# Both context units at the head of a bidirectional DeltaNet scan, and the context projection between its passes, on one Trainium2 core

## The chip, the core and the metric

The kernel runs on one core of a Trainium2 chip. The core has five engines with a queue of instructions each: TensorE (PE, matrix products; its weight loads are listed apart as PEld), VectorE (DVE), ScalarE (ACT), GpSimd (POOL) and SyncE (SP). Each engine takes its own queue in order and waits on semaphores for the others. All loads and stores between memory and the core's SBUF are issued on SP's queue, one behind the other. The metric is the device time of one execution in microseconds (us).

## The reference

One layer of a hybrid backbone over two sequences: 128 context tokens and 2048 latent tokens, width 1024, 4 heads of 128. Cut to what matters (the function names are those of the reference):

```python
def gated_delta_chunked(q, k, v, g, beta, s0):          # per head, chunks of 64 tokens
    ...
    sol = lax.linalg.triangular_solve(a_mat + jnp.eye(DN_CHUNK, dtype=f32), rhs, ...)
    ...
    def step(S, xs):
        qd, kd, u_c, w_c, qk_c, gl = xs
        v_new = u_c - jnp.einsum('bhck,bhkv->bhcv', w_c, S)
        o = jnp.einsum('bhck,bhkv->bhcv', qd, S) + jnp.einsum('bhcs,bhsv->bhcv', qk_c, v_new)
        S = S * jnp.exp(gl)[..., None, None] + jnp.einsum('bhck,bhcv->bhkv', kd, v_new)
        return S, o
def mixer(h, s0, ...):
    ...
    o_a, s_new = delta_bidir(q, k, v, g2, beta2, s0)     # o_forward + flip(o_backward)
    o_a = rmsnorm(o_a, o_norm_l) * jax.nn.silu(gate.reshape(B, T, H_A, DV))
    u = jax.nn.gelu(u)
    vg = layernorm_noaffine(jax.nn.gelu(vg).reshape(B, n_chunks, CHUNK_MLP, G_B, C_B))
    mixed = jnp.einsum('gts,bnsgc->bntgc', ws_l, vg) + bs_l.T[None, None, :, :, None]
    o_b = u * mixed.reshape(B, T, D_B).astype(u.dtype)
    out = jnp.concatenate([o_a.reshape(B, T, D_A).astype(h.dtype), o_b.astype(h.dtype)], axis=-1)
    return out @ w_out_l, s_new
def block(x, s0, mod, n_chunks, ...):
    h = rmsnorm(x, norm_mix_l) * (1.0 + sc1) + sh1
    o, s_new = mixer(h, s0, n_chunks, ...)
    x = x + ga1 * o
    h = rmsnorm(x, norm_ffn_l) * (1.0 + sc2) + sh2
    x = x + ga2 * (jnp.square(jax.nn.relu(h @ w_ff1_l)) @ w_ff2_l)
    return x, s_new
```

The context starts both directions from a zero state and its two final states are an output. The latents start each direction from a given state (`state_delta`), so the context's scan and the latents' scan do not depend on each other. The context's layer output is an output too.

## The kernel before

The 2176 tokens are 17 tiles of 128 (`NT`): tile 0 is the context, tiles 1 to 16 are the latents. Products that need full precision are made of three matrix products (`mm3`, lines 217 to 219): a factor is split into a high half H, cast on ACT, and a low half L, the difference, taken on DVE; the three are H x H, H x L and L x H. For weights the cast is line 191 and the difference line 192; line 190 scales the raw weight where it has a scale.

The kernel has three phases.

The first, to about 455 us, makes the modulation, the normed input, the projections to q, k and v, the convolution, and writes q, k, v, the products of k with k and q with k, the gates' exponents and the two halves of the input to memory.

The second, the scan, from about 455 to about 1294 us, is where the change is. It works on 34 units, each one tile in one direction. Before the change their order is: tiles 0 to 16 forward (units 0 to 16), tile 0 backward (unit 17), tiles 16 down to 1 backward (units 18 to 33). A unit has

- loads: `prep_loads` (gb, the row of exponents, by line 935; KK and QK), issued about three units ahead, and `scan_loads` (kT, qT, kt, vt, eg);
- a preparation (`prep`), which needs nothing of other units: the decay masks E and Es (ACT lines 977 and 978, two selects on POOL), KK (DVE line 990, POOL line 992), its half-precision copy AH (ACT line 995), X (DVE lines 996, 997), Y, the transpose of X (PE line 1003, copied by ACT on line 1005), and then five rounds of doubling the inverse, each of which is PE line 1025 (from Y), P on DVE (line 1029), PE lines 1038 and 1040 (from P), and copies of Y and X on ACT (1041, 1042). P has its fixed part written from `identq` (line 1028) in the units of tile 0 only, since later units of the same direction overwrite the same half;
- a chain step (`scan`) that hangs on the state S of the unit before: kt scaled (ACT 1093), vt, vn, the new state (`quad` on line 952, then line 1119 on DVE), and the output o (lines 1129 to 1136). A forward unit stores o to memory, a backward unit adds the stored forward part.

Both of the context's units and the first latent unit of each direction begin anew: behind units 0 and 17, `after` stores the context's final state and loads `state_delta` into a buffer of S, of which there are two.

Between the matrix products of units stand fillers. In the forward pass they are the rest of the mixer for each tile (`f2_steps`): the gate projection "g", and the gMLP's "v" and "u" (8 weight blocks of three products each, 24 products for a tile and part, tile "pm"/"pj"), their activation functions (from line 1159; the gate is computed on ACT and DVE and stored), the statistics, and the spatial product (line 1213 and its neighbours). The gates of the first four tiles (`HT`) are made before the scan. Weights of v and u are loaded and split about then too. In the backward pass the fillers are the output projection of the tile just finished (`o_steps`: norm, lines 1265 to 1273; transposes, 1286; the halves oH and oL; 48 products with the weights `w_out`, in tile "pj"; the residual, 1309 and 1310) and, for tiles above 8, the normed input of the MLP. `w_out` is loaded, scaled and split in 16 pieces near the end of the forward pass, in times 17.58 to 18.3.

The order is written down as events with a time, in units: `at(time, step)` sets one, `spread` spaces several evenly, and unit i's steps lie around time i. The events are sorted by time and emitted. A filler's first product is held behind the latest chain or preparation product. A planner then sets each engine's order with its own costs, so that the written times and the order on an engine agree only roughly. `NF` is the number of filler steps that are put ahead of the scan instead of being spread, at times -12 and -8; before the change it is 46. The fillers' sequence is: gates of tiles 0 to 3; v and u of tiles 0 to 3; g, v and u of tiles 4 to 14; then the last two tiles. Each step's inputs hH and hL are loaded one visit ahead. Staging tiles for weights come from a pool of four ("raw", `NS`); `part` is a temporary of the MLP's input, five buffers.

The third phase, from about 1294 us, is the MLP with weights combined on the fly and streamed (lines 1431 and 1437). The change does not touch it.

## Time and profile before

| | us |
|---|---|
| median of 3 runs | 2711.76 |
| fastest, slowest run | 2704.84, 2714.13 |
| profiled execution: device time | 2707.53 |
| profiled execution: span of the trace | 2705.8 |
| PE busy in the span | 2632.3 (97%) |
| DVE busy | 1868.0 (69%) |
| ACT busy | 1246.1 (46%) |

PE's busy time by stage, from windows of the trace:

| stage | length, us | PE busy, us | DVE busy, us | granted PE clock |
|---|---|---|---|---|
| first phase, 0 to 455 | 455 | 445.78 | 297.37 | 1.00 |
| forward pass, 455 to 914 | 459 | 439.12 | 347.81 | 0.98 |
| around the turn, 914 to 959 | 45 | 41.22 | 39.00 | 0.89 |
| backward pass, 959 to 1294 | 335 | 318.89 | 268.51 | 0.99 |
| MLP, 1294 to 2705 | 1411 | 1387.31 | 915.27 | 0.99 |

How to read a profile line: "L1025" is line 1025 of the kernel, followed by the engine, the operation, the tile written <- the tiles read, and the shape. A line of waits reads "engine, tile, line <- what it waited for: idle us in all, how often, longest". In a line of time order the first number is the start in us, the second the duration, and in square brackets stands the idle time ahead with what ended it. The granted clock is the share of full speed that PE was given: at 0.5 the same product takes twice as long. Busy time of PE at a low clock is therefore time lost as well.

### The profile page before, as it was taken

What the parts mean: (1) busy time and instruction counts of PE and PEld (TensorE: products, weight loads), DVE (VectorE), ACT (ScalarE), POOL (GpSimd) and SP (SyncE); (2) the same over time, 40 slices, a digit from 0 to 9 for tenths busy, and PEclk for the clock granted to TensorE, in tenths of its full rate; (3) what the DMA queues carried; (4) which work ended last, traced back from release to release, by engine and by line L of the source; (5) the groups of instructions that cost most, each with busy time, mean ns of one, the idle gap of its engine ahead of it and who ended that gap; (6) DMA issues with size and microseconds to landing.
All of it is one profiled execution on the core that took longest, in us unless ns stands there. A gap on an engine that the chain in (4) does not pass through costs nothing.

```text
span 2705.8 us, 45189 instructions
## 1 busy us (share of the span) xinstructions
PE 2632.3 (97%) x15698; PEld 2196.5 (81%) x15698; DVE 1868.0 (69%) x3909; ACT 1246.1 (46%) x3092; POOL 228.2 (8%) x448
## 2 busy tenths in 40 slices
PE   8999998999999999999999999999999999999998
PEld 5999997788887787778888778888888787788887
DVE  5867656877777978985677857565565556775874
ACT  4655555555555667763355533332342432232441
POOL 3111213111111111110000000000000000000000
PEclk9999999999999999999999999999999999999999
DMA  8867539555555657875887786433459979776772
GB/s 296 279 199 223 185 115 294 179 159 155 163 162 172 212 180 245 268 263 175 286 234 232 213 299 206 123 102 109 117 174 371 326 262 308 267 239 216 233 258 91
DMA packets 569387, 580.91 MB, mean 215 GB/s; under 512 B 35692, under 2 KB 401692, under 8 KB 565574
## 3 DMA queue, kind: packets, MB, share of 16 engines
q1 hardware_dynamic: 569158, 578.03, 66.5%
q8 instruction: 123, 2.02, 0.3%
q14 instruction: 106, 0.87, 0.1%
HBM read 398.14 MB, written 179.74 MB: 214 GB/s over the span
## 4 chain that ended last, share of the span: by engine, by line
PE 82%; DMA 7%; DVE 6%; issue 2%; ACT 2%; SPq 1%; POOL 0%; DVEq 0%; POOLq 0%; ACTq 0%
PE f L219 16%; PE f L217 16%; PE f L218 16%; PE pj L217 6%; PE pj L219 6%; PE pj L218 6%; PE pd L952 3%; PE pm L217 1%; DMA qT<-qT_d 1%; PE pm L218 1%; PE pm L219 1%; PE pt L568 1%; PE pd L1129 1%; PE pd L1130 1%; PE pt L528 1%
## 5 line engine op out<-in xcount | busy, mean ns | idle before, releaser
L219 PE MATMUL f<-hop,zL 128*128 128x512 f32 x960 | 377.9, 394 | 1.7 <-DVE zL L1431 1.7
L217 PE MATMUL f<-hop,zH 128*128 128x512 f32 x960 | 377.6, 394 | 1.2 <-ACT zH L1437 1.2
L218 PE MATMUL f<-hop,zH 128*128 128x512 f32 x960 | 378.0, 394 | 0.0
L217 PE MATMUL f<-hop,wH 128*128 128x512 f32 x896 | 356.2, 398 | 5.8 <-ACT wH L1437 5.8
L219 PE MATMUL f<-hop,wL 128*128 128x512 f32 x896 | 352.2, 393 | 0.0
L218 PE MATMUL f<-hop,wH 128*128 128x512 f32 x896 | 352.0, 393 | 0.0
L1437 ACT CAST zH<-zraw 128x512 fp32r<-128x512 f32 x240 | 147.1, 620 | 299.2 <-DVE zraw L1431 91.9
L219 PEld LDWEIGHTS f<-hop,zL 128*128 128x128 f32 x960 | 180.9, 188 | 45.0 <-DVE zL L1431 3.5
L217 PEld LDWEIGHTS f<-hop,zH 128*128 128x128 f32 x960 | 180.7, 188 | 44.7 <-ACT zH L1437 2.9
L218 PEld LDWEIGHTS f<-hop,zH 128*128 128x128 f32 x960 | 180.6, 188 | 40.9
L1431 DVE TENSOR_TENSOR zL<-zraw,zH 128x512 fp32r<-128x512 f32 x240 | 162.6, 687 | 68.2 <-ACT zH L1437 50.8
L217 PEld LDWEIGHTS f<-hop,wH 128*128 128x128 f32 x896 | 169.4, 189 | 40.9 <-ACT wH L1437 6.2
L219 PEld LDWEIGHTS f<-hop,wL 128*128 128x128 f32 x896 | 169.0, 189 | 38.0 <-DVE wL L1431 0.3
L218 PEld LDWEIGHTS f<-hop,wH 128*128 128x128 f32 x896 | 169.4, 189 | 35.2
L217 PE MATMUL pj<-kH,wH 128*128 128x386 f32 (+2 forms) x568 | 191.0, 339 | 0.3 <-DVE kH L466 0.3
L219 PE MATMUL pj<-kH,wL 128*128 128x386 f32 (+2 forms) x568 | 190.6, 336 | 0.0
L218 PE MATMUL pj<-kL,wH 128*128 128x386 f32 (+2 forms) x568 | 189.8, 334 | 0.0
L176 POOL TENSOR_TENSOR r<-rsq,nhalf 128x1 f32<-128x1 f32 (+1 forms) x38 | 23.6, 621 | 1516.4 <-DVE rsq L175 1516.4
L1431 DVE TENSOR_TENSOR wL<-raw,wH 128x512 fp32r<-128x512 f32 x112 | 76.1, 687 | 76.0 <-ACT wH L1437 75.0
L516 DVE SCALAR_TENSOR_TENSOR cv<-pj,vec,cv 128x384 f32<-128x384 f32 (+2 forms) x164 | 87.1, 539 | 59.9 <-ACT cv L513 58.5
L217 PEld LDWEIGHTS pj<-kH,wH 128*128 128x128 f32 x568 | 107.5, 190 | 4.8 <-issue 4.2
L217 PE MATMUL pj<-wH,hH 128*128 128x512 f32 x248 | 110.1, 444 | 0.0
(398 smaller groups left out, 6090.2 us busy)
## 6 DMA issues: line engine op xcount, KB each, us to landing
zraw<-z_d SPq DMA_DIRECT2D x212, 256.0 KB
raw<-in_w_ff_dram SPq DMA_DIRECT2D x128, 256.0 KB
hop<-hop_d SPq DMA_DIRECT2D x28, 1024.0 KB
z_d<-c SPq DMA_DIRECT2D x96, 256.0 KB
zraw<-s_d SPq DMA_DIRECT2D x96, 256.0 KB
raw<-in_w_mod_dram SPq DMA_DIRECT2D x80, 256.0 KB
r<-in_w_ff_dram SPq DMA_DIRECT2D x80, 256.0 KB
s_d<-s SPq DMA_DIRECT2D x64, 256.0 KB
```

What stands on the lines that cost most here:

```text
L176: G.tensor_tensor(out=out, in0=t[:np_, :n], in1=nhalf[:np_, :n], op=ALU.pow)
L217: T.matmul(ps, lh, rh, start=first and i == 0, stop=False, skip_group_check=more)
L218: T.matmul(ps, lh, rl, start=False, stop=False, skip_group_check=more)
L219: T.matmul(ps, ll, rh, start=False, stop=last and i == n - 1, skip_group_check=more)
L516: V.scalar_tensor_tensor(out=cv[:, o : o + m], in0=ps[:, s + sh : s + sh + m], scalar=convw[:, w, j : j + 1], in1=cv[:, o : o + m], op0=AL ...
L528: T.transpose(pq[:, i * P : (i + 1) * P], u["x2"][:, i * P : (i + 1) * P], ident)
L568: T.matmul(ps[:, i * P : (i + 1) * P], kTt[:, i * P : (i + 1) * P], rhs[:, i * P : (i + 1) * P], start=True, stop=True)
L952: T.matmul(p[:, h, :], lhs[:, h, :], rhs[:, h, :], start=True, stop=True)
L1129: T.matmul(p[:, h, :], u["qT"][:, h, :], s[:, h, :], start=True, stop=False)
L1130: T.matmul(p[:, h, :], u["QK"][:, h, :], u["vn"][:, h, :], start=s is None, stop=True)
L1431: V.tensor_tensor(out=out, in0=a, in1=b, op=op)
L1437: A.copy(h, src)
```

## The change

- The order of units becomes: tile 0 forward, tile 0 backward, tiles 1 to 16 forward, tiles 16 to 1 backward. `unit` gets two flags: `fresh` (units 0, 1, 2 and 18) writes the fixed part of P anew, because the direction turns there; `last` (tile 16 forward, tile 1 backward) leaves out the state update, whose result nobody reads.
- Tile 0's forward output stays in SBUF; its backward unit adds it and stores the sum, which the output projection loads again.
- `after` only stores the two context states; `first_state` loads `state_delta` for units 2 and 18. S has three buffers instead of two, `part` four instead of five.
- The context's output projection (`o_loads`, `o_steps` of unit 1) is written at 17.3 to 18.8, between the passes; it was at 17 to 19.66, as that of unit 17.
- The fillers' sequence becomes: gates of tiles 0 to 3; gates, then v, then u of tiles 4 and 5; g, v and u of tiles 6 to 14; v and u of tiles 0 to 3; the last two tiles as before. `NF` becomes 62. The loads of tile 4's and 5's input are at -11.5 and -9.5, the loads of unit 0 at -12.5 instead of -10.

```diff
-NF = 46
+NF = 62
...
-        def unit(t, d):
+        def unit(t, d, fresh=False, last=False):
...
-                    if t == 0:
+                    if fresh:
                         V.tensor_copy(pms[s], identq)
...
                 s = u["s"]
+                if last:
+                    return
                 p = pd()
                 quad(p, u["kt"], u["vn"])
-                sn = q32("S", 2)
+                sn = q32("S", 3)
...
-                o = q32("o", 2)
-                if d == 0:
+                u["o"] = o = q32("o", 2)
+                if t == 0 and d:
+                    V.tensor_tensor(out=o, in0=p, in1=units[0]["o"], op=ALU.add)
+                    store(out=of_d[0:P, :].rearrange("p (h d) -> p h d", h=H), in_=o)
+                elif d == 0:
                     A.copy(o, p)
+                    if t == 0:
+                        return
...
-        units = [unit(t, 0) for t in range(NT)] + [unit(t, 1) for t in [0] + list(range(NT - 1, 0, -1))]
+        units = [unit(0, 0, True), unit(0, 1, True)] + [unit(t, 0, t == 1, t == NT - 1) for t in range(1, NT)]
+        units += [unit(t, 1, t == NT - 1, t == 1) for t in range(NT - 1, 0, -1)]
...
-            return fp.tile([P, 512], F32, tag="part", name=name, bufs=5)
+            return fp.tile([P, 512], F32, tag="part", name=name, bufs=4)
...
+            if t == 0:
+                u["o"] = u["of"].rearrange("p (h d) -> p h d", h=H)
...
         def after(i):
 
-            d = 0 if i == 0 else 1
-            store(out=new_state[0, 0, d].rearrange("h k v -> k h v"), in_=units[i]["sn"])
-            s0 = q32("S", 2)
+            store(out=new_state[0, 0, i].rearrange("h k v -> k h v"), in_=units[i]["sn"])
+
+        def first_state(i, d):
+            units[i]["s0"] = s0 = q32("S", 3)
             load(out=s0, in_=state_delta[0, 0, d].rearrange("h k v -> k h v"))
-            units[i + 1]["s0"] = s0
...
-            at(i - 3 if i > PL else -10, u["prep_loads"])
+            at(i - 3 if i > PL else -12.5, u["prep_loads"])
...
-            if i >= NT:
+            if i > NT:
                 at(i, lambda u=u: o_loads(u))
...
-        for n, (t, gi) in enumerate([(t, "g") for t in range(HT)] + [(t, gi) for t in range(HT) for gi in "vu"]
-                                    + [(t, gi) for t in range(HT, NT - 2) for gi in "gvu"]
+        visits = [4, 5] + list(range(6, NT - 2)) + list(range(HT)) + [NT - 2, NT - 1]
+        after_visit = dict(zip(visits, visits[1:]))
+        for n, (t, gi) in enumerate([(t, "g") for t in range(HT)] + [(t, gi) for gi in "gvu" for t in (4, 5)]
+                                    + [(t, gi) for t in range(6, NT - 2) for gi in "gvu"]
+                                    + [(t, gi) for t in range(HT) for gi in "vu"]
                                     + [(NT - 2, "g"), (NT - 1, "g")]
                                     + [(t, gi) for t in (NT - 2, NT - 1) for gi in "vu"]):
...
-        at(-9, f2[0][0])
+        at(-11.5, f2[4][0])
+        at(-9.5, f2[5][0])
...
+        at(1, lambda: first_state(2, 0))
+        at(NT + 0.5, lambda: first_state(NT + 1, 1))
+        at(NT + 0.3, lambda: o_loads(units[1]))
+        first, second = o_steps(units[1])
+        spread(NT + 0.8, NT + 1.1, first, "fill")
+        spread(NT + 1.1, NT + 1.8, second, "fill")
```

More of the change, by code (lines that the diff above doesn't have):

```diff
@@ L1136, in _ @@
                     V.tensor_tensor(out=o, in0=p, in1=u["of"].rearrange("p (h d) -> p h d", h=H), op=ALU.add)
-                    u["o"] = o
             u["t"], u["d"] = t, d
@@ L1336, in g @@
                 if "s" not in u:
-                    u["s"] = None if i in (0, NT) else units[i - 1]["sn"] if i not in (1, NT + 1) else u["s0"]
+                    u["s"] = None if i < 2 else units[i - 1]["sn"] if i not in (2, NT + 1) else u["s0"]
                 f()
@@ L1357, in hybrid_step @@
             spread(i + w[2], i + w[3], [scan_step(i, f) for f in u["scan"]], "chain")
-            if i in (0, NT):
+            if i < 2:
                 at(i + w[2] + (w[3] - w[2]) * 0.7, lambda i=i: after(i))
-            if i >= NT:
+            if i > NT:
                 at(i, lambda u=u: o_loads(u))
@@ L1375, in hybrid_step @@
             main, later = f2[t][1][gi]
-            if gi == "v" and t + 1 < NT - 1 or gi == "g" and t == NT - 2:
-                flat.append((KT * n - 0.5, f2[t + 1][0]))
+            if gi == "v" and t not in (4, 5, NT - 2, NT - 1) or (t, gi) in ((5, "u"), (NT - 2, "g")):
+                flat.append((KT * n - 0.5, f2[after_visit[t]][0]))
             flat += [(KT * n + j, st) for j, st in enumerate(main)]
```

## The prediction

> **What bounds the kernel now.** I read the page first, then the stage windows, the waits of PE, and the orders in time of PE, ACT, DVE, POOL and SP around the two places that the windows single out.
>
> ```profile
> span 2705.8 us, 45189 instructions
> PE 2632.3 (97%) x15698; PEld 2196.5 (81%) x15698; DVE 1868.0 (69%) x3909; ACT 1246.1 (46%) x3092; POOL 228.2 (8%) x448
> 500.00:850.00 350.00, 344.62 (x2948) 285.26 (x2947) 258.53 (x745) 190.09 (x508) 44.61 (x58) 1.00 0.52 161
> 461.00:464.50 3.50, 1.16 (x7) 0.56 (x6) 3.16 (x6) 3.50 (x9) 1.66 (x2) 1.00 1.07 374
> 464.50:482.30 17.80, 10.50 (x56) 6.71 (x56) 15.20 (x40) 11.51 (x31) 7.47 (x6) 0.52 0.85 288
> 914.30:933.50 19.20, 16.54 (x147) 14.54 (x145) 18.84 (x59) 13.23 (x41) 3.90 (x5) 0.73 0.54 173
> 919.75:922.50 2.75, 1.08 (x21) 0.80 (x21) 2.75 (x8) 2.75 (x13) 0.51 (x1) 1.00 1.04 335
> 922.50:933.00 10.50, 9.50 (x77) 8.72 (x77) 10.14 (x40) 4.79 (x16) 3.39 (x5) 0.51 0.40 125
> 933.00:940.00 7.00, 6.14 (x71) 5.59 (x69) 6.94 (x21) 5.69 (x20) 0.00 (x0) 1.00 0.56 169
> ```
>
> PE is busy 97% of the span, so only its idle time, its slow time and removed work can be won. The windows list busy time of PE, weight loads, DVE, ACT, POOL, then the granted PE clock and the DMA share. The long forward stretch loses 350 - 344.6 = 5.4 us in 350. Two places lose far more. At the **start of the scan** (461 to 482.3) PE idles 2.34 + 7.30 us, and its 10.50 busy us run at clock 0.52, so 10.50 x 0.48 = 5.0 us are lost on speed: 14.7 us. At the **turn between the passes** (919.75 to 940) idle is 1.67 + 1.00 + 0.86 and the slow clock costs 9.50 x 0.49 = 4.7: 8.2 us. The change touches both.
>
> ```profile
> PE pd L1025 <- ACT Y L1005: 2.8, 1, 2.8
> PE pd L1038 <- DVE P L1029: 2.3, 3, 1.2
> PE pd L1025 <- ACT Y L1041: 1.0, 1, 1.0
> PE pm L218 <- DVE wL L192: 1.9, 2, 1.6
> PE pm L217 <- ACT wH L191: 1.8, 1, 1.8
> 460.51 0.39 PE L218 MATMUL pm<-wL,hH 128*128 128x512 f32 x1
> 460.74 0.39 PE L219 MATMUL pm<-wH,hL 128*128 128x512 f32 x1
> 463.97 0.40 PE L1003 MATMUL pd<-ident,X 128*128 128x128 f16 x4 [0.59 <-DVE X L997]
> 471.75 0.37 PE L1025 MATMUL pd<-Y,As 128*128 128x64 f16 x4 [2.77 <-ACT Y L1005]
> ```
>
> At the start PE waits for weight halves of the v and u projections (L191, L192: 3.7 us) and for the first units' own chains (Y and P: 6.1 us).
>
> **The change part by part.** *Head of the fillers.* NF goes from 46 to 62. The planner's list for the changed kernel has 72 filler matmuls between the head gates and the first L1003: the gates of tiles 4 and 5 and v of tile 4. The old list has 22 there, of v of tile 0, and PE had done 21 by 461.1. So 51 remain; they start 0.23 us apart (460.51, 460.74) and last 51 x 0.228 = 11.6 us, and PE has done L1003 at about 461.1 + 11.6 + 0.2 = 472.9. They need no weights of u and only the last of v. But the next PE instruction, L1025, needs Y, and ACT's list puts eleven steps between the second AH and the copy of Y: four casts of weights, E and its exponential for two units, the gate of tile 4, kt, and a third AH. I walk it with these rows.
>
> ```profile
> 454.07 0.52 SPq L935 DMA_DIRECT2D gb<-g_d  x1
> 459.52 1.28 ACT L977 ACTIVATE E<-gb,gcol 128x128 f32<-128x128 f32 x4 [7.75 <-DMA gb<-g_d]
> 464.43 1.13 DVE L990 SCALAR_TENSOR_TENSOR KK<-KK,beta,Es 128x128 f32<-128x128 f32 x4
> 458.49 0.64 POOL L992 TENSOR_SCALAR_AFFINE_SELECT KK<-KK 128x512 f32<-128x512 f32 x1 [5.77 <-DMA hL<-hL_d]
> 465.63 3.77 POOL L992 TENSOR_SCALAR_AFFINE_SELECT KK<-KK 128x512 f32<-128x512 f32 x1 [1.99 <-DMA QK<-qk_d]
> 469.43 0.62 ACT L995 CAST AH<-KK 128x512 f16<-128x512 f32 x1 [3.81 <-POOL KK L992]
> 471.60 0.59 ACT L1159 ACTIVATE gw<-pm 128x512 f32<-128x512 f32 x1
> 472.09 0.62 ACT L978 ACTIVATE E<-E 128x512 f32<-128x512 f32 x1
> 472.61 1.27 ACT L1093 ACTIVATE kt<-kt,eglg 128x128 f32<-128x128 f32 x4
> 478.39 0.61 ACT L191 CAST wH<-raw 128x512 fp32r<-128x512 f32 x1
> 469.05 1.71 SPq L182 DMA_DIRECT2D raw<-in_w_in_dram  x3
> ```
>
> gb of the second unit is issued at the same place of SP's queue as before, so it lands at 459.5 again (5.4 us after issue). E and its exponential end near 461.4, Es on POOL near 462.3, KK on DVE near 463.7. POOL's L992 took 0.64 us with DVE idle and 3.77 us with DVE running tensor-tensor work; DVE has such work until about 466, so I let it end at 466.5. Then ACT: AH 0.6, a cast 0.6, E 1.3, the gate 0.6, exp 0.6: 470.2. The third unit's two selects on POOL (0.7 each), QK (0.7) and KK (1.1) on DVE and KK on POOL (0.7) end near 474.1; AH to 474.7, three casts 1.8, E 1.3, exp 0.6: Y is copied at 478.4 and ready at 478.9. The raw weights, issued near 469, need 5.4 us too and are there at 475. So PE waits 6.0 us in one piece, then about 2 us in the rounds of P and Y that follow (before: 2.3 for P, 1.0 for Y), and the clock falls again; about 7 us of busy time at half speed cost 3.5. That is 11.5 us lost instead of 14.7: **3.2 us won**. Ends: L992 held to 3.77 for the third unit too makes Y 3.1 us later (0.1 won), with a longer slow time 2 us lost; Y ready when PE arrives makes the loss 2 + 3.5, so 9.2 won. I take the walk, which uses the row of each step.
>
> [...]
>
> *Context units first.* Units 0 and 1 are now the two directions of tile 0; the prep chains are as independent as those of tiles 0 and 1 were. P is reset where the direction turns, for four units instead of two: ten more copies on DVE. The last units of both passes drop the state update.
>
> ```profile
> L1028 DVE COPY P<-identq x10: 277/283/294, 447.2 to 858.0; 128x512 f16<-128x512 f16 x10
> 930.73 1.10 DVE L1119 SCALAR_TENSOR_TENSOR S<-S,egl,pd 128x128 f32<-128x128 f32 x4
> 905.97 1.05 PE L952 MATMUL pd<-vn,kt 128*128 128x128 f32 x8
> ```
>
> 10 x 0.283 = 2.8 us come to DVE and 2 x 1.10 leave it: taken as nothing; the copies lie beside fillers at the start, and without that cover cost up to 2.8. On PE 2 x 1.05 = **2.1 us** of L952 go, between 0 (both in stretches that DVE holds) and 2.1. The store of the sum and its reload replace the store and load that unit 17 had. The load of tile 16's forward output now follows its own store by less than one unit; a unit is some 20 us long (914.3 to 933.5 is one), against 5.4 us from issue to landing at a DMA share over 1.0, so nothing is taken for it; if it came late, the loads behind it on SP would wait with it. The fifth buffer of part goes, and with its wait could hold one load on SP in the backward pass: between 0 and one landing, taken 0. Filler work in the forward pass is thinner by 48 matmuls over 20 units, 0.5 us each; PE stays the longer engine there (344.6 busy against DVE 258.5), so 0, at most 2.
>
> *Projection between the passes.* The hole at the turn exists because the fillers end while DVE is full (18.84 of 19.20 us).
>
> ```profile
> 919.51 0.40 PE L219 MATMUL pj<-wH,hL 128*128 128x512 f32 x1
> 937.72 0.47 PE L217 MATMUL pj<-wH,oH 128*128 128x512 f32 x1
> L190 DVE TENSOR_SCALAR raw<-raw,wscale x12: 477/484/490, 881.6 to 916.5; 128x512 f32<-128x512 f32 x12
> L192 DVE TENSOR_TENSOR wL<-raw,wH x16: 675/682/692, 876.4 to 920.6; 128x512 fp32r<-128x512 f32 x16
> ```
>
> In the old list the unit that ends at 933.5 has 12 filler matmuls and its successor 60, 48 of them the context projection, from 937.7. In the changed list the same two units hold 60 and 0: the projection comes one unit earlier, and the hole moves behind it and is bare. For the bare unit I take the old one less 12 x 0.228 and one spatial product of 1.0: PE content 16.54 x 0.73 - 3.7 = 8.4 us. By the old rows DVE has some 15 us in it, and the chain adds waits: 16.5 us long, 8.1 lost. Ahead of the projection lies a stretch with 19 us on DVE (eleven of P, As, X at 0.41, five groups of four at 1.1, four weight halves at 0.68, two scalings at 0.48, the rest 6) and 10 us on PE; fillers that were ahead and the projection that follows it without DVE take up half of the difference: 4.4 lost. Together 12.5 against 8.2: **4.3 us given back**. Ends: 0, if DVE's work slides under the 48 matmuls of the projection, and 10, if it cannot. PE's list also has the last three L190/L192 results in front of everything behind them; each is one more wait for DVE.
>
> From about 1040 us on the lists of all engines are nearly the old ones, so nothing else is priced.
>
> **Sum** against the profiled execution of 2707.53 us: - 3.2 + 4.3 - 2.1 = - 1.0, so 2706.5, given as 2706. The median of the three runs, 2711.76, is 4.2 above that execution, and the runs reach from 2704.84 to 2714.13, a spread of 0.34%; I therefore call 0.3% (8 us) what a measurement tells.
>
> **The rivals.** *The start is really covered.* PE arrives nearly 9 us later at L1003 than it did (463.97); if POOL's L992 runs at 0.64 and the casts do not queue, Y is there: 9.2 won, the turn gives back 1, L952 2.1: 2707.5 - 10.3 = 2697. For it: the v and u waits (3.7 us) go in any case. Against it: the eleven steps of ACT, which nothing in the trace lets run faster than in the walk but the one POOL row.
>
> *The turn gets worse (slower).* One mechanism: the projection stands in PE's queue ahead of the chain, and its last weights are scaled and split by a full DVE; the chain of both units then waits, and the bare unit follows at half clock. With nothing won at the start it decides from 8.2 + 2.1 = 10.3 us lost there; with 10 given back, none won at the start and L952 hidden, the time is 2717. For it: DVE 10.14 of 10.50 busy; against it: the old projection had no such waits worth naming, and the weights were complete at 920.6, before it.
>
> *It does not do what it says*: the stall at the start only changes its name, from weights to Y. That is half of my forecast already.
>
> **How the numbers follow.** Forecast, both ends cancel to within 8 us: 0.38. Start covered, 2697 or so: 0.34 with all cases below 2699.4. Turn worse, 2717 or so: 0.28 with all cases above 2715.6. The chances of faster, same and slower are these. The ends of the terms add to -11.3 and +16.8, 2696 to 2724; the fastest run shown lies 2.7 below the profiled execution, which lowers the lower end to 2693. The upper terms hardly all fall together: 2692 to 2721 leaves out 2 in 10. The forecast's own range is 2699 to 2715.
>
> **What would show it.** Right: no wait of PE for L191 or L192 near 461 to 472; one wait of 4 to 8 us at L1025 for Y of L1005; a clock near 0.5 after it; 48 projection matmuls (oH, oL) ahead of a unit with no filler; a clock row below 1.00 behind the projection. Wrong at the start if that wait is under 2 us; wrong at the turn if the bare unit keeps the clock at 1.00, or if PE waits for L192 inside the projection by more than 3 us.

## The result and the profile after

The changed kernel takes 2716.95 us (median of 22 runs, 2711.30 to 2724.32) against 2711.34 us for the kernel before (22 runs, 2704.84 to 2717.54): a ratio of 1.0018 with a 95% interval of 1.0010 to 1.0026. It is some 5 us slower, a change inside the 0.3% that the prediction called no change, but clear of zero and on the other side of it than the forecast of 2706. The profiled execution took 2717.36 us, its span is 2715.6.

The page of the changed kernel begins so:

```profile
span 2715.6 us, 45142 instructions
PE 2631.7 (97%) x15682; PEld 2195.9 (81%) x15682; DVE 1867.8 (69%) x3911; ACT 1247.8 (46%) x3092; POOL 226.4 (8%) x448
```

PE's busy time is that of before (2632.3), the span is 9.8 us longer; so the time lies in idle PE. These are windows of the trace after, with the columns of the prediction's first fence (length; busy PE, weight loads, DVE, ACT, POOL; granted clock; DMA share):

```profile
473.00:479.50 6.50, 0.09 (x3) 0.01 (x1) 4.20 (x9) 4.41 (x11) 1.55 (x3) 0.91 0.99 341
479.50:493.00 13.50, 11.52 (x72) 8.54 (x72) 12.26 (x31) 6.80 (x17) 1.32 (x2) 0.67 0.77 263
500.00:850.00 350.00, 338.99 (x2925) 279.81 (x2924) 258.39 (x747) 192.31 (x518) 43.75 (x58) 1.00 0.53 156
871.70:878.40 6.70, 3.75 (x31) 2.93 (x30) 1.06 (x3) 4.67 (x12) 0.00 (x0) 0.94 0.57 197
878.40:884.00 5.60, 5.58 (x23) 4.24 (x23) 5.60 (x13) 1.89 (x4) 3.50 (x3) 0.50 0.82 240
900.00:940.00 40.00, 34.65 (x309) 27.77 (x308) 36.54 (x108) 25.19 (x65) 7.27 (x9) 1.00 0.65 201
940.00:952.30 12.30, 12.30 (x104) 10.31 (x103) 9.67 (x21) 4.92 (x14) 0.00 (x0) 1.00 0.67 218
952.30:971.00 18.70, 12.87 (x118) 11.62 (x115) 12.68 (x36) 10.74 (x37) 3.13 (x4) 0.63 0.68 218
```

Four things are to be seen. At the start, 473 to 493, PE idles 6.41 + 1.98 us and loses 11.52 x 0.33 = 3.8 on speed, 12.2 us in all; in the same stretch of work the kernel before lost 14.7 (and 0.6 more up to 490). The forward stretch 500 to 850, which idled 5.4 us before, idles 11.0. There is a hole behind 871 that was not there: 2.95 us of idle time and 5.58 x 0.50 = 2.8 at half clock. And the turn: 5.35 idle from 900 to 940, and 5.83 idle with 12.87 x 0.37 = 4.8 slow behind the projection, which fills 940 to 952 without a gap.

Idle time and time lost to the clock, summed over windows of ten us, by stage and for the profiled executions of both kernels. Time lost to the clock is busy time times one less the granted clock. That reads a little high: products of one form start 0.43 us apart at 0.50 (881.10, 881.52, 881.95 and 882.38 in the trace after) and 0.23 us apart at 1.00 (885.15, 885.39, 885.62 and 885.85), 1.9 times and not twice.

| stage, us | before: idle + slow | after: idle + slow | difference |
|---|---|---|---|
| 440 to 520 (start) | 11.7 + 5.1 | 8.4 + 3.8 | -4.6 |
| 520 to 860 (forward) | 6.0 + 0.0 | 12.6 + 0.0 | +6.6 |
| 860 to 900 | 0.8 + 0.0 | 3.0 + 3.0 | +5.2 |
| 900 to 1000 (turn) | 5.1 + 4.1 | 11.6 + 5.6 | +8.0 |
| 1000 to 1300 (backward) | 16.1 + 1.4 | 14.5 + 0.0 | -3.0 |

The sum is +12.2; less the 2.1 of products that are left out it is 10.1, and the profiled span grew by 9.8. The medians differ by less, 5.6.

PE's waits of the trace after in the stretches 455 to 500 and 520 to 860 (engine, tile, line <- what it waited for: us, times, longest):

```profile
PE pd L1025 <- ACT Y L1005: 6.4, 1, 6.4
PE pd L1038 <- DVE P L1029: 1.5, 2, 1.3
...
PE pd L1038 <- DVE P L1029: 8.4, 11, 1.5
PE pd L1025 <- ACT Y L1041: 3.9, 4, 1.6
```

The last two, of the forward pass, were 4.3 and 1.5 before:

```profile
PE pd L1038 <- DVE P L1029: 4.3, 7, 1.2
PE pd L1025 <- ACT Y L1041: 1.5, 2, 0.9
```

### The profile page after: what moved, and what is told of

Read it like the earlier page. It is cut to its first block, busy times and chain, and to the rows that moved or that the text cites. A ratio compares the mean times of both kernels' runs of the same rounds, so it can differ in the third digit from the quotient of the medians.

```text
span 2715.6 us, 45142 instructions
## 1 busy us (share of the span) xinstructions
PE 2631.7 (97%) x15682; PEld 2195.9 (81%) x15682; DVE 1867.8 (69%) x3911; ACT 1247.8 (46%) x3092; POOL 226.4 (8%) x448
## 4 chain that ended last, share of the span: by engine, by line
PE 82%; DMA 7%; DVE 6%; issue 2%; ACT 1%; SPq 1%; POOL 0%; DVEq 0%; POOLq 0%; ACTq 0%
PE f L219 16%; PE f L217 16%; PE f L218 16%; PE pj L217 6%; PE pj L219 6%; PE pj L218 6%; PE pd L952 2%; DMA qT<-qT_d 2%; PE pm L217 1%; PE pm L219 1%; PE pm L218 1%; PE pd L1131 1%; DMA raw<-in_w_mod_dram 1%; PE pd L1132 1%; PE pt L568 1%
## 5 line engine op out<-in xcount | busy, mean ns | idle before, releaser
L218 PEld LDWEIGHTS pj<-kL,wH 128*128 128x128 f32 x568 | 107.5, 189 | 0.5
```

Of the source, the lines that this page charges most:

```text
L218: T.matmul(ps, lh, rl, start=False, stop=False, skip_group_check=more)
```

## The experiments

Runs on one chip share its runs of the kernel before, and chips differ by a few us (the medians of the kernel before on the five chips of the experiments are 2708.35 to 2712.23); so each is given with its ratio to the kernel before on the same chip, and as that ratio in us (ratio less one, times 2711). The intervals are 4 to 8 us wide.

**The three parts, each undone or alone.** The first four kernels take the change apart into the order of units (with its flags and buffers), the place of the context projection, and the fillers' sequence with NF.

Old fillers in the changed kernel (e1):

```diff
-NF = 62
+NF = 46
...
-        visits = [4, 5] + list(range(6, NT - 2)) + list(range(HT)) + [NT - 2, NT - 1]
...
+        for n, (t, gi) in enumerate([(t, "g") for t in range(HT)] + [(t, gi) for t in range(HT) for gi in "vu"]
+                                    + [(t, gi) for t in range(HT, NT - 2) for gi in "gvu"]
```

> The changed kernel with the fillers' sequence and NF of the kernel before (46 steps, v and u of tiles 0 to 3 first); the units' order and the place of the context projection stay changed. Theory A (the place of the projection and the late hole near 871 us cost, the fillers' new sequence wins at the start): slower than the changed kernel by some 4 us, near 2721, with the waits for L191 and L192 back at 461 to 472. Theory B (the new sequence thins the forward pass, and that is what costs): PE's idle time between 520 and 860 falls from 12.6 to about 6 us and the hole near 871 goes; the start costs 4.6 more; in sum some 7 us faster than the changed kernel, near 2710.

Measured: 2701.66 us, ratio 0.9961 (0.9945 to 0.9976), -10.6 us. Theory A fell: the new sequence wins nothing, it costs. B was right on the side, and its size was too small.

Old place of the projection in the changed kernel (e2):

```diff
-        at(NT + 0.3, lambda: o_loads(units[1]))
+        at(NT, lambda: o_loads(units[1]))
         first, second = o_steps(units[1])
-        spread(NT + 0.8, NT + 1.1, first, "fill")
-        spread(NT + 1.1, NT + 1.8, second, "fill")
+        spread(NT + 1.36, NT + 1.64, first, "fill")
+        spread(NT + 1.66, NT + 2.66, second, "fill")
```

> The changed kernel with the context projection written at 18.36 to 19.66 again (its loads at 17), where it was before. Theory A: the 17.2 us lost between 900 and 1000 fall back to about 9, and the hole near 871 goes too if it came from the projection's loads: 8 to 13 us faster than the changed kernel, 2704 to 2709. Theory B: the turn alone changes, at most 4 us faster, near 2713, and the idle time of the forward pass stays at 12 us. Should the bare unit merely move again, the time stays at 2717.

Measured: 2714.34 us, ratio 1.0007 (0.9996 to 1.0019), +1.9 us, 3 us faster than the changed kernel. The forward pass idles 13.4 us as it did (B).

New fillers alone (e3): the kernel before with NF, the fillers' sequence and the loads of tiles 4 and 5 from the change.

```diff
-NF = 46
+NF = 62
...
+        visits = [4, 5] + list(range(6, NT - 2)) + list(range(HT)) + [NT - 2, NT - 1]
...
-        at(-9, f2[0][0])
+        at(-11.5, f2[4][0])
+        at(-9.5, f2[5][0])
```

> The kernel before with the fillers' new sequence and NF of 62 alone; units and projection as before. Theory A: the start wins 3 to 5 us, nothing else moves: 2707. Theory B: the forward pass loses 6 to 12 us in small waits for P and Y and perhaps a hole near 870, the start wins 4: 2713 to 2719.

Measured: 2725.41 us, ratio 1.0048 (1.0033 to 1.0063), +13.0 us. More than either theory had; the profile has what B said, without the win at the start (12.4 + 4.0 us lost from 440 to 520):

```profile
520.00:860.00 340.00, 328.75 (x2835) 272.48 (x2834) 250.63 (x725) 185.05 (x495) 42.73 (x57) 1.00 0.54 161
860.00:900.00 40.00, 36.34 (x291) 28.61 (x290) 30.60 (x84) 21.45 (x55) 4.86 (x5) 0.96 0.59 185
```

The order of units alone (e4): the edits of the first two kernels together.

```diff
-NF = 62
+NF = 46
...
-        spread(NT + 1.1, NT + 1.8, second, "fill")
+        spread(NT + 1.66, NT + 2.66, second, "fill")
```

> The changed kernel with the old fillers and the old place of the projection: of the change only the order of the units (with its flags and buffers) is left. Theory A and B: two groups of eight L952 products and two state updates less, start and turn as before: 2709 to 2711. If the time is 2715 or more, the order of units itself costs (the second state's load, P's copies, four buffers of part), which neither theory has.

Measured: 2703.30 us, ratio 0.9967 (0.9953 to 0.9980), -8.9 us, faster than both theories said. Its windows, to be held against those of the fillers alone:

```profile
520.00:860.00 340.00, 336.15 (x2876) 278.50 (x2874) 252.28 (x729) 185.43 (x504) 43.39 (x57) 1.00 0.52 158
860.00:900.00 40.00, 40.00 (x323) 30.95 (x321) 35.16 (x93) 25.45 (x66) 6.44 (x7) 1.00 0.68 216
```

So the parts, in us against before:

| | old fillers, NF 46 | new fillers, NF 62 |
|---|---|---|
| old order of units | 0 | +13.0 |
| new order, projection at its old place | -8.9 | +1.9 |
| new order, projection between the passes | -10.6 | +4.9 |

The fillers cost 13.0, 10.8 and 15.5 us, whatever stands beside them. The order of units wins 8.9 and 11.1. The projection's place gives -1.7 and +3.0, nothing that these intervals separate from zero. The change is a win of some 9 us and a loss of some 13 that nearly cancel.

**The number ahead, or the sequence.** NF and the sequence were then set apart. The changed kernel with NF at 46 alone (e5):

```diff
-NF = 62
+NF = 46
```

> The changed kernel with NF at 46: the new sequence of fillers, but no more of them ahead of the scan than before. Theory C (amount: the 16 steps, 48 products, that are taken from the forward pass thin its cover): PE's idle time between 520 and 860 falls from 12.6 to about 5, the hole of 860 to 900 goes, 2704 to 2708. Theory D (sequence: with the gates of 4 and 5 made early and v and u of tiles 0 to 3 left for last, the end of the pass holds only DVE-heavy fillers): the idle time stays at 11 to 13 and the hole stays, 2714 to 2718.

Measured: 2706.44 us, ratio 0.9982 (0.9972 to 0.9992), -4.9 us; the forward pass idles 3.8 us (C).

The changed kernel with the old sequence, NF staying at 62 (e6):

```diff
-        visits = [4, 5] + list(range(6, NT - 2)) + list(range(HT)) + [NT - 2, NT - 1]
...
+        for n, (t, gi) in enumerate([(t, "g") for t in range(HT)] + [(t, gi) for t in range(HT) for gi in "vu"]
```

> The changed kernel with the old sequence of fillers, but 62 steps ahead of the scan. Theory C: the forward pass idles 11 to 13 us as in the changed kernel; at the start PE waits for the weights of v and u, 4 us more; 2716 to 2720. Theory D: forward idle 4 to 6, no hole near 870, 2701 to 2706.

Measured: 2719.20 us, ratio 1.0028 (1.0017 to 1.0039), +7.6 us. The time is C's; the forward idle time is neither's, 7.2 us where C had 11 to 13 and D 4 to 6.

The changed kernel with v and u of tiles 0 to 3 ahead of tiles 6 to 14 (e7):

```diff
-        visits = [4, 5] + list(range(6, NT - 2)) + list(range(HT)) + [NT - 2, NT - 1]
+        visits = [4, 5] + list(range(HT)) + list(range(6, NT - 2)) + [NT - 2, NT - 1]
...
-                                    + [(t, gi) for t in range(6, NT - 2) for gi in "gvu"]
                                     + [(t, gi) for t in range(HT) for gi in "vu"]
+                                    + [(t, gi) for t in range(6, NT - 2) for gi in "gvu"]
```

> The changed kernel, 62 steps and the gates of 4 and 5 first, but v and u of tiles 0 to 3 right behind v and u of tiles 4 and 5 instead of behind tile 14. Theory C: forward idle and hole stay as they are, 2715 to 2719. Theory D: the hole of 860 to 900 (6 us) goes since tiles with gates stand there again, and the idle time of 700 to 860 falls from 7.7 to about 4: 2706 to 2710, while the idle time of 520 to 700 rises by 1 to 3.

Measured: 2715.04 us, ratio 1.0009 (0.9999 to 1.0020), +2.4 us. The hole stays (5.1 us idle from 860 to 900), as theory C said; the forward idle fell to 8.3, which C had not.

C, the amount, holds: from 46 to 62 the time rises by 18 us with the old sequence and by 10 with the new. The sequence is not free of effect: at 46 the new one reads 5.7 us slower than the old, at 62 2.7 us faster, both at the edge of the intervals or inside them. Two more values of NF show the shape, and that fewer is no better. The first is with the old sequence (e9):

```diff
-NF = 62
+NF = 38
```

> The changed kernel with the old sequence and only 38 steps ahead of the scan (46 gave 2701.7, 62 gave 2719.2). Theory C1 (a unit takes some 22.8 us whatever stands between, so a step ahead of the scan only shifts the scan): the eight steps are 24 products of 0.23 us, 5.5 us; the first output o comes 4 to 5.5 us earlier and the end with it, as far as the start does not idle more: 2697 to 2700, and units of 22.8 us again. Theory C2 (at 46 the forward pass is bound by PE already): units get longer by 0.2 to 0.3 us, the start idles more, 2702 to 2706.

Measured: 2709.48 us, ratio 0.9988 (0.9978 to 0.9997), -3.3 us: C2, and worse than it said. The second is with the new sequence (e10):

```diff
-NF = 62
+NF = 54
```

> The changed kernel with 54 steps ahead, between the 46 that gave 2706.4 and the 62 that gave 2717. Theory C1: half way, the first o some 4 us later than with 46, 2710 to 2713. A threshold instead (fillers that run out at one place, near 870): at 2706 to 2708 or at 2715 to 2717.

Measured: 2713.64 us, ratio 1.0000 (0.9991 to 1.0009): between 46 (-4.9) and 62 (+4.9), with no threshold.

**What paces the forward pass.** "Thin cover" stands in the next texts for one reading: PE waits inside each round of the inverse, filler products hide those waits, and with fewer of them the waits show. First DVE's work: the centring left out (line 1213 of the changed kernel; the result then lacks the normalisation of v), in the changed kernel with its 62 steps (e11) and in the kernel with old fillers and 46 (e12).

```diff
             def center():
                 vg = u["vg"]
-                for g in range(4):
-                    V.tensor_scalar(out=vg[:, g * P : (g + 1) * P], in0=vg[:, g * P : (g + 1) * P],
-                                    scalar1=u["mv"][:, g, 0:1], scalar2=u["rs"][:, g : g + 1],
-                                    op0=ALU.subtract, op1=ALU.mult)
+                return
```

> The changed kernel without the centring of the gMLP's v (line 1213, four operations on DVE for each tile, 1.1 us, 17 tiles; the normalisation of v is left out), with PE's work the same. Theory G (DVE's queue sets the wait for P, so DVE paces the units): PE's idle time between 520 and 860 falls from 12.6 to 7 or less, the units get shorter by 0.3 to 0.5 us, 2705 to 2711. Theory H (the rounds' own latency and late loads pace them): idle stays at 11 to 13, units at 22.7 to 22.9, 2714 to 2718.

Measured: 2707.90 us, ratio 0.9987 (0.9978 to 0.9996), -3.5 us, which is 8.4 faster than the changed kernel. The time is G's; the forward idle fell to 10.4 only, where G had 7 or less, and a unit takes 22.65 us for 22.87.

> The kernel of e1 (changed units and projection, old sequence, 46 steps) without the centring on line 1213; the normalisation of v is left out, PE's work is the same. At 62 steps this gave 9 us. Thin cover (DVE's work sets waits only where PE has too little between the rounds): at 46 it gives 3 us at most, 2699 to 2702. DVE paces the units in any case: 8 to 9 us again, 2692 to 2694.

Measured: 2701.31 us, ratio 0.9970 (0.9962 to 0.9979), -8.1 us; with the centring it was -10.6. By the totals DVE's work is worth 8 us at NF 62 and nothing at 46, as thin cover asks. But the pass itself does not show that difference: its fifteen units (table below) get 3.3 us shorter at 62 and 2.3 at 46, for 13.8 and 11.5 us less work on DVE. The rest of both totals arises outside the pass, so this pair does not tell thin cover from its rival.

Then PE's work, 48 products put into the pass for nothing, at 62 (e13) and with old fillers at 46 (e14):

```diff
+                    if gi == "u" and k == 0 and t > 0:
+                        mm3(u[gi], [(hH[k], hL[k], wh, wl)])
                     mm3(u[gi], [(hH[k], hL[k], wh, wl)], first=k == 0, last=k == KT - 1)
```

> The changed kernel with three more products at the head of u of each latent tile (the first block's, done once for nothing and then written over): 48 products, 10.9 us of PE work, laid evenly into the forward pass, in place of the 48 that NF took out of it. Thin cover: PE's idle time between 520 and 900 takes them in, 2716 to 2720. PE-bound pass: 2726 to 2729.

Measured: 2730.43 us, ratio 1.0082 (1.0068 to 1.0096), +22.2 us, 17 more than without. By its total, thin cover fell; PE's idle time from 520 to 900 took in 5.0 of the 10.9 us.

> The kernel of e1 with the same 48 extra products. With 46 steps ahead the forward pass idles only 5 us, so nearly all of the 10.9 us must show by thin cover as by a PE-bound pass: 2709 to 2713. If it stays under 2706, PE's time in the forward pass is no bound even here.

Measured: 2732.72 us, ratio 1.0090 (1.0076 to 1.0104), +24.4 us: 35 more than without, three times the work added. No theory had that, and the cause is open.

The totals hold more than the forward pass. These windows are the pass alone, from the first output o to the sixteenth, fifteen units: of the changed kernel, and in the next fences of the kernel with old fillers, of 48 products more at 62, and of 48 more at 46.

```profile
529.10:872.20 343.10, 330.55 (x2855) 273.85 (x2853) 253.97 (x741) 188.71 (x511) 43.86 (x58) 1.00 0.53 159
```

```profile
520.90:863.80 342.90, 337.77 (x2885) 279.74 (x2884) 253.99 (x732) 188.82 (x512) 44.41 (x58) 1.00 0.52 158
```

```profile
530.70:876.30 345.60, 337.43 (x2886) 279.25 (x2884) 253.70 (x741) 188.51 (x512) 43.98 (x58) 1.00 0.52 158
```

```profile
519.50:878.50 359.00, 347.72 (x2923) 287.34 (x2922) 255.30 (x731) 189.78 (x513) 43.33 (x57) 1.00 0.50 151
```

The same for these and others, with the filler products counted in the traces (a few records are missing):

| kernel | products up to the first o | products in fifteen units | fifteen units, us |
|---|---|---|---|
| new fillers alone | 297 | 802 | 341.1 |
| no centring, 62 | 297 | 806 | 339.8 |
| projection at its old place | 297 | 807 | 343.7 |
| changed kernel | 297 | 808 | 343.1 |
| v and u early, 62 | 291 | 814 | 339.4 |
| old sequence, 62 | 275 | 832 | 341.4 |
| new sequence, 46 | 265 | 834 | 337.5 |
| new sequence, 54 | 269 | 838 | 344.0 |
| 48 more, 62 | 306 | 840 | 345.6 |
| before | 247 | 847 | 344.3 |
| no centring, 46 | 249 | 847 | 340.7 |
| old fillers (46) | 247 | 849 | 343.0 |
| order of units alone | 247 | 853 | 343.3 |
| old sequence, 38 | 237 | 856 | 345.8 |
| 48 more, 46 | 253 | 885 | 359.0 |

From 802 to 856 products, 12.3 us of PE work at 0.228 (from 936.50 to 941.51 in the trace after 22 products start 0.228 us apart), the fifteen units take 337.5 to 345.8 us with hardly a trend; 32 products more at 62 lengthened them by 2.5 us for 7.3 us of work. Only the row with 885 is longer, by far more than its work. In this range a product taken out of the forward pass does not shorten it.

How the total of the run with 48 more at 62 came about, by marks against the changed kernel: sixteenth o +4.1, twentieth +3.9, last o +9.0, span +13.5. Two thirds of it arise in the backward pass and the MLP, into which the edit put nothing. Why is open.

**The late loads.** In the hole and at the turn DVE waits for a load (5.75 us for qT, 3.48 for QK) with P behind it in its queue. First an attempt to take one such wait from the head of the queue (e8):

```diff
-                    if s == 2:
+                    if s == 4:
                         V.tensor_tensor(out=u["QK"], in0=u["QK"], in1=u["E"], op=ALU.mult)
```

> The changed kernel with the product of QK and E on DVE written one round later (behind s = 4 instead of s = 2). Theory E (DVE's waits for the loads of QK, 8.8 us between 520 and 860 and 3.5 near 953, stand in its queue ahead of P, and PE's waits for P come from them): those waits of DVE fall under 2 us, PE's idle time between 520 and 860 falls by 3 to 5 and the bare unit near 950 loses 3 less: 2708 to 2712. Theories C and D: DVE's waits go, PE's waits stay within 2 us: 2715 to 2719.

Measured: 2718.19 us, ratio 1.0018 (1.0007 to 1.0028), +4.9 us, nothing gained. But DVE's waits for QK in the forward pass only fell from 8.8 to 7.9 us, so the edit did not do what the test needed; it tells nothing on E.

Then two stores of SP's queue, moved to POOL's, in the changed kernel (e16) and in that with old fillers (e17):

```diff
-                store(out=gate_d[t * P : (t + 1) * P, :], in_=th)
+                nc.gpsimd.dma_start(out=gate_d[t * P : (t + 1) * P, :], in_=th)
...
-                store(out=ob_d[t * P : (t + 1) * P, :], in_=ob)
+                nc.gpsimd.dma_start(out=ob_d[t * P : (t + 1) * P, :], in_=ob)
```

> The changed kernel with the fillers' two stores (the gate, and the gMLP's output ob) issued on POOL's queue instead of SP's. Theory S (stores that wait for DVE hold the loads behind them on SP): DVE's waits of 5.75 us for qT near 877 and of 3.5 us for QK near 957 fall under 2, the stretch 860 to 900 loses under 2 us instead of 6 and the turn 3 to 4 less: 2706 to 2710. Theory T (the loads are late because their buffers come free late): the waits stay: 2714 to 2719. POOL's own selects may come later behind the stores, up to 1 us for a unit at the start.

Measured: 2717.93 us, ratio 1.0034 (1.0022 to 1.0045), +9.2 us. DVE's two waits, in the trace of this kernel:

```profile
875.08 0.69 DVE L1095 TENSOR_TENSOR qT<-qT,gb 128x512 f32<-128x512 f32 x1 [4.26 <-DMA qT<-qT_d]
...
954.39 0.69 DVE L1044 TENSOR_TENSOR QK<-QK,E 128x512 f32<-128x512 f32 x1 [2.48 <-DMA QK<-qk_d]
```

They shrank by 1.5 and 1.0 us and did not go; the stretch 860 to 900 loses 4.9 us, the turn 15.6, where they lost 6.0 and 17.2 in the changed kernel, and the total is no shorter. So these two stores are at most a small part of the cause. That the buffers come free late (T) is what is left; no run made them free earlier.

> The same two stores on POOL's queue in the kernel of e1 (46 steps, old sequence), which has no hole near 871. Theory S: only the turn can gain, 2 to 4 us, 2698 to 2700. Theory T: 2700 to 2704.

Measured: 2704.22 us, ratio 0.9989 (0.9978 to 1.0000), -3.0 us: by its ratio 7.6 us worse than without (-10.6), by its median just above T's range. S fell here too.

**The bare unit.** The unit behind the projection has no fillers; here the projection's products are spread over it, in the kernel with old fillers (e15):

```diff
-        spread(NT + 1.1, NT + 1.8, second, "fill")
+        spread(NT + 1.1, NT + 2.5, second, "fill")
```

> The kernel of e1 with the products of the context projection spread from 18.1 to 19.5 instead of 18.1 to 18.8. If the loss at the turn (8.4 idle and 4.3 slow) is that of the bare unit behind the projection, spreading covers it: it falls by 4 to 6, 2696 to 2698. If the loss is DVE's full queue and late loads, it stays within 2: 2700 to 2704.

Measured: 2704.33 us, ratio 0.9975 (0.9964 to 0.9986), -6.8 us, for -10.6 without. The turn did what the first theory said. Windows of 900 to 1000 and 1000 to 1300, first of the kernel with old fillers, then of this one:

```profile
900.00:1000.00 100.00, 91.59 (x772) 75.29 (x770) 84.65 (x223) 58.72 (x174) 14.75 (x18) 0.95 0.55 180
1000.00:1300.00 300.00, 287.59 (x2323) 236.22 (x2322) 237.49 (x581) 178.76 (x543) 36.48 (x44) 1.00 0.75 243
```

```profile
900.00:1000.00 100.00, 96.30 (x856) 79.09 (x856) 86.10 (x234) 64.95 (x197) 16.46 (x20) 0.97 0.60 196
1000.00:1300.00 300.00, 281.25 (x2205) 229.22 (x2204) 231.02 (x563) 171.20 (x513) 35.52 (x42) 0.98 0.71 229
```

The loss at the turn halves, from 8.4 + 4.6 to 3.7 + 2.9 us. The backward pass then idles 18.8 us instead of 12.4 and has a slow stretch; all is given back. These two kernels have the same list on PE up to the turn, and yet the first o stands at 520.9 in one trace and at 515.0 in the other: a mark of one execution is good to some six us, while the length of fifteen units agrees within one (343.0 and 343.7).

Of the kernels that compute the whole result, the one with old fillers has the lowest ratio (2701.66 us, five runs): it beats the kernel before by 0.24 to 0.55%, and the changed kernel too.

## Why the prediction was wrong, step by step

**Head of the fillers: right, to half a us at its ends.** Rows of the trace after for the walk:

```profile
472.68 0.40 PE L1003 MATMUL pd<-ident,X 128*128 128x128 f16 x4
...
479.49 0.37 PE L1025 MATMUL pd<-Y,As 128*128 128x64 f16 x4 [6.41 <-ACT Y L1005]
...
464.97 2.84 POOL L992 TENSOR_SCALAR_AFFINE_SELECT KK<-KK 128x512 f32<-128x512 f32 x1 [1.00 <-DVE KK L990]
...
474.42 0.64 POOL L992 TENSOR_SCALAR_AFFINE_SELECT KK<-KK 128x512 f32<-128x512 f32 x1 [1.85 <-DVE KK L990]
...
478.86 0.57 ACT L1005 CAST Y<-pd 128x512 f16<-128x512 f32 x1
```

L1003 began at 472.68 (its end was put at 472.9), Y was copied at 478.86 (478.4), PE waited 6.41 us in one piece (6.0), and no wait for L191 or L192 is left. Lost: 12.2 against 11.5; won: 3.1 of 3.2 up to 493, and 4.6 up to 520. Inside the walk two steps came later than walked, the first L992 ended at 467.81 (466.5) and the third unit's at 475.06 (474.1), and what follows took 3.8 us for 4.3, so a part of the close fit is luck. The 7 us of busy time at half speed were the author's estimate, with no row beside it; PE was busy 7.0 us between 478.3 and 488.5, by windows of one us. The rival that the start is really covered fell. What the walk left out is what the experiments found: this win is inside the part of the change that costs 13.

**Forward pass: this is the step that failed.** It said that the pass becomes thinner by 48 products, that PE stays the longer engine there, "so 0, at most 2". That weighs busy times over 350 us, and such averages say nothing of the rounds: PE waits for P and Y inside the rounds, 8.4 and 3.9 us in all in the pass after and 4.3 and 1.5 before. With 297 products instead of 247 ahead of the first o, 11.4 us of work are done before the scan. They bought 4.6 us of lost time there, and the fifteen units behind became 1.2 us shorter. The idle time of the pass rose by 6.6, and a hole of 5.2 opened behind it: together the size of the work moved. The stages differ from the forecast by 11.1 us in sum (+10.1 for -1.0), and these 11.8 are that: the turn lost 3.7 more than forecast, and the start and the backward pass made that up.

Which part is at fault is shown: the kernels with 46, 54 and 62 steps, two with the old sequence and three with the new, get slower with the number ahead. By what way is less sure. The fifteen units hardly get shorter when products leave them: in the table, without the two kernels that lack the centring, the three with 802 to 808 products take 342.6 us on average and the four with 847 to 856 take 344.1, 1.5 us for 10.4 us of work. Thin cover fits that, and so does a pass that the rounds themselves pace, whatever fillers stand between them. In this range PE's busy time does not set the length, nor does DVE's alone: 13.8 us less work on DVE shortened it by 3.3. The runs leave open which of the two it is: with 48 products more at 62 the pass kept to both and the total to neither, the same at 46 lost three times its work, and at 38 the time rises again, for which the pass (856 products, 345.8 us) explains 3 us of 7.

The hole behind 871 in the trace after, by order of release:

```profile
870.36 1.28 ACT L977 ACTIVATE E<-gb,gcol 128x128 f32<-128x128 f32 x4
...
871.66 0.32 SPq L935 DMA_DIRECT2D gb<-eg_d  x1
872.07 0.52 SPq L964 DMA_DIRECT2D qT<-qT_d  x1
...
877.34 0.69 DVE L1095 TENSOR_TENSOR qT<-qT,gb 128x512 f32<-128x512 f32 x1 [5.75 <-DMA qT<-qT_d]
...
878.42 0.37 PE L1038 MATMUL pd<-P,X 128*128 128x64 f16 x4 [2.98 <-DVE P L1029]
```

SP issues the next gb as ACT ends reading one of its three buffers, qT stands behind it on SP, DVE can go on 5.3 us after its issue, and P stands behind qT in DVE's queue. From 860 to 900 every kernel at NF 62 loses 3.8 to 6.0 us, idle and slow together; the kernel before and four with old fillers at 46 lose under 1, two more with old fillers at 46 lose 1.6 and 1.8. The kernel before:

```profile
860.00:900.00 40.00, 39.16 (x324) 31.18 (x322) 33.49 (x86) 25.99 (x67) 4.54 (x6) 1.00 0.59 195
```

That the load causes the hole is read from one trace; no run took the wait away.

**Context units first: the mechanism was thought worth 2.1 us and the runs give 8.9.** The eight products of each of the two L952 groups are gone (256 for 272). Most of the rest shows before the first o, which stands at 517.9 for the order of units alone and at 524.1 before, with the same 247 products ahead; by the spread of such marks that can't be divided further, and why it is so much is open. The copies of P and the fourth buffer of part, priced at nothing, were not run apart; the kernel that has them wins 8.9.

**Projection between the passes: right in its form, wrong in its size, and of no weight.** The projection runs from 936 to 947.7, PE busy 11.53 of 11.70 us and DVE 9.20, a bare unit follows at a granted clock of 0.63 on average from 952.30 to 971.00, PE waited 1.5 us for oL inside the projection, and the hole was put at 4.4 + 8.1 us: it is 5.35 + 10.6. It was wrong on what holds the bare unit. DVE was to have 15 us of work in it; it has 12.68 in 18.70 us and stands still for a load:

```profile
949.96 0.39 PE L1132 MATMUL pd<-vn,QK 128*128 128x128 f32 x2
...
951.25 0.32 SPq L959 DMA_DIRECT2D QK<-qk_d  x1
...
956.92 0.69 DVE L1044 TENSOR_TENSOR QK<-QK,E 128x512 f32<-128x512 f32 x1 [3.48 <-DMA QK<-qk_d]
...
958.00 0.37 PE L1038 MATMUL pd<-P,X 128*128 128x64 f16 x4 [2.02 <-DVE P L1029]
```

The last product that reads a buffer of QK ran at 949.96, behind the projection in PE's queue; the load into it was issued 1.3 us later, and DVE went on 5.7 us after that. Putting 48 products ahead of the chain's output holds its buffers some 11 us longer, an estimate (48 x 0.228), and with them the loads: that was not priced. But the load is a part of the loss only. In the kernel with old fillers the projection stands at the same place, DVE waited 0.84 us for QK there (at 963.03), and the turn still lost 12.7 us, for 17.2. Spreading the products took half of that away. And yet the place of the projection moved no total beyond its interval. With spread products the backward pass gave back all that the turn had won; with old fillers the turn loses the same at both places (13.1 at the old one). "Nothing else is priced" behind 1040 was therefore wrong too: it lost 17.5 us before, and 12.1 to 25.0 in the kernels here.

**The rivals.** That the turn decides (2717) has the time right and the reason wrong: it asked for 10.3 us lost at the turn with nothing won at the start; 8.0 were lost there, and the forward pass and its hole lost 11.8. No rival had the forward pass. The range of 2692 to 2721 holds the time because the turn's upper end stood in for it; that is luck. The upper end of the sum, +16.8, also leaves out the one landing (5.4 us) that the text allows for the fourth buffer of part.

**The signs.** All that were named for being right came: no wait for L191 or L192 near 461 to 472, one wait of 6.41 us for Y, a low clock behind it, 48 products of the projection ahead of a unit without fillers, and a low clock behind those. None of them looked at the forward pass, so they could all come while the time moved the other way.

## What to carry to other kernels

Filler work that stands between the rounds of a dependent chain is not free to move ahead of it. Price such a move by what the stretch gives back as well as by the wait that it fills: here 11.4 us moved ahead filled 4.6 us, and the fifteen units gave back 1.2. A busy share of 98% on PE over a long stretch does not show that the stretch gets shorter when work leaves it; the length of a fixed number of units with more and with fewer products does. When a change has several parts, run each alone, since here a win of 9 us and a loss of 13 looked like nothing.

## What the runs showed of the hardware

The clock's way back differs from place to place. After the hole PE was busy without a gap from 878.42 on and still had 0.50 in the whole window up to 884.00; the clock was back at 884.5, 6 us after the restart. At the start the last gap ended at 484.23 and the clock was back at 488.5, 4.3 us later. Windows of one us give the moments, here those of the hole (0.81 and 0.77 are a fall at 877.6 and a return at 884.5) and of the start (0.63 and 0.75 are a fall at 478.3 and a return at 488.5):

```profile
877.00:878.00 1.00, 0.00 (x0) 0.00 (x0) 0.66 (x2) 0.00 (x0) 0.00 (x0) 0.81 1.06 408
884.00:885.00 1.00, 1.00 (x8) 0.48 (x7) 0.82 (x3) 0.00 (x0) 0.55 (x1) 0.77 0.97 361
478.00:479.00 1.00, 0.00 (x0) 0.00 (x0) 1.00 (x2) 1.00 (x3) 0.49 (x1) 0.63 1.10 388
488.00:489.00 1.00, 1.00 (x4) 0.77 (x4) 1.00 (x4) 0.00 (x0) 0.00 (x0) 0.75 0.88 311
```

The stretch at half clock is 6.8 us long after the hole, 10.2 at the start (478.3 to 488.5) and 17.1 at the start before the change (465.3 to 482.4, from 0.65 in the window 465 to 466 and 0.82 in 482 to 483). What sets these lengths was not shown.

POOL's select on L992 took 2.84 us at 464.97, while DVE ran tensor-tensor work to 467.3, and 0.64 at 474.42 with DVE waiting. Before the change the two prices were 3.77 (at 465.63) and 0.64 (at 458.49). Tensor-tensor work on DVE did not always go with a high price: in the trace after the select took 0.64 us at 907.52 too, with L1168 and L192 on DVE beside it.
